# A hybrid SSD backbone on one core: SSD layer ends with the norm factor in PSUM and sums on TensorE, low parts on VectorE alone, step widths a unit later, projections first

## The chip, the cores and the metric

The kernel runs on one core of one Trainium2 chip. The metric is the device time of one execution in microseconds (us); a comparison uses the median of several runs. Five engines work side by side, each through its own queue in order: TensorE (PE, with its weight load PEld), VectorE (DVE), ScalarE (ACT), GpSimd (POOL) and SyncE (SP), which here issues the DMAs of the weights. An engine waits at a semaphore until what it needs is there, and whatever stands behind the waiting instruction on that engine waits too.

## What is computed

The reference is a backbone of four layers with 256 latent and 256 context tokens of width 1024. Each layer modulates a normalised input, runs a mixer (layer 0 and 3: SSD; 1: gMLP; 2: retention), adds it back with a gate, and does the same with a SwiGLU FFN. The context is carried through the first three layers and read, but not written, by the last. Of layer 0's and 3's mixer this matters here:

```python
def rmsnorm(x, g):
    y = xf * lax.rsqrt(jnp.mean(xf * xf, axis=-1, keepdims=True) + EPS)
    return (y * g).astype(x.dtype)
...
z, xbc, dt = jnp.split(h @ w_in, [SSD_INNER, SSD_INNER + SSD_CONV_DIM], axis=-1)
xbc = jax.nn.silu(dwconv(xbc, conv_w, conv_b))
dt_f = jax.nn.softplus(dt[..., :SSD_HEADS] + dt_bias_f)      # the step widths
...
y = y + d_skip * xs                                            # after the scans
y = y.reshape(...) * jax.nn.silu(z)                            # the gate
return rmsnorm(y, norm_g) @ w_out
```

What follows the mixer in every layer is `x = x + g1 * o`, then `modulate(rmsnorm(x, norm2_g), sh2, sc2)` into the FFN.

## The kernel before

**Tiles and products.** Activations lie with the feature on the partition and the token along the row: `X` holds 8 blocks (m = 0 to 7) of 128 features by 512 tokens, the context in columns 0 to 255, the latents from T = 256 on. Every product in float32 is made as three matmuls of a reduced form: a high part `AH` and a low part `AL` of the input, `whi` and `wlo` of the weight; `mm3` issues hi x hi (L307), lo x hi (L308) and hi x lo (L309). A *unit* is one weight block of 128 x 1024 (some of 768): SyncE brings it as `st` (512 KB), ScalarE casts it to `whi` (L227), and a subtraction gives `wlo` (L228). This subtraction runs on VectorE, or on GpSimd for every fourth unit (`POOL_SHARE`, `share[0]`; `boundary` sets other shares by its argument `pool_share`): 372 and 130 units of 502 where the tile is `wlo`. Four units are held in parts at a time. A unit needs 24 matmuls: 8 blocks times three.

**Jobs and quanta.** A job is one unit's matmuls and the evacuation of its PSUM tile. In `boundary`, which joins two stages, the last product of a mixer is cut into quanta of 12 matmuls over 256 tokens, one for each block m of the context (k = 0 to 7) and then of the latents (k = 8 to 15), so that norm, sums and evacuation can be written between them. All PSUM tiles come from one ring of eight banks.

**A norm.** `Norm.add` squares a block of X on ScalarE (L520, L532), and adds it to `nacc` (L526) on GpSimd, the late ones on VectorE. `rms_steps` then makes the factor in three steps: `s0` sums over the partitions on TensorE (L484), takes the mean on VectorE (L488) and the power -1/2 on GpSimd (L489); `s1` puts it on a diagonal `dg` (L494, VectorE); `s2` broadcasts it with a matmul of ones (L498). `Norm.steps` applies it, block by block: a product on VectorE (`t1k`, L557), ScalarE's `AH` (L567), VectorE's `AL` (L551); for the context's m = 0, 2, 4 GpSimd makes AL (L565).

**An SSD layer** (`ssd`, a function inside the kernel's scope) opens with the units of `dt`, B, C and x. `a1` transposes the step widths' input `DX` on TensorE (L865; `dx` is its name); `a2` starts with two VectorE steps (L875, L876) and then runs the softplus as a chain of 21 GpSimd steps (L877 to L889), whose last but one writes `SF` in the trace's names; `dtb` turns it into decays with TensorE's L897, L899, L903. `conv_evac` makes the 5-tap convolutions (ScalarE L821, VectorE L824, four passes) and SiLU (L833). Then four groups follow. In group g, the windows of `WINDOWS` set the order of projections x (for group g+1), z units, and `o` units (the out product of the group before, whose input `yg` comes from the gate: L1061 on TensorE, L1065 and L1072 on VectorE, L1077 on ScalarE, L1089 and L1090), and `scan_slots` puts the scan's steps between them.

**An SSD layer's end.** The sum of squares of the gated y is known only with group 3. So `out_last` computes the out product without the factor, `o_whole` adds it to the earlier groups' part (L1155), `rms_steps` makes the factor `rb`, `rsink` copies it to a tile `th` (L1206, ScalarE), and `o_norm` applies it: `X * g * rb` (L1165, VectorE), then adds the saved x (`back`, L1166, VectorE), then `fin_norms[a].add`. `last.after` says behind which quantum k each of these stands.

**The V scaling of gMLP** (L1264) multiplies the normalised V on VectorE; TensorE's spatial product L1283 waits for it.

Of the kernel before, what the change touches and what calls it, by code (L numbers as in the profile page):

```python
# [16 lines left out]
P = 128  # L17
# [13 lines left out]
POOL_SHARE = 4  # L31

PAD_W, PAD_H = 24, (48, 32)
# [37 lines left out]
class Job:  # L71
# [14 lines left out]
    True: ("zxxzxzxzxx", "oxoxozoxzxzxzx", "oxoxozoxzxzxzx", "zzzozooo"),  # L86
    False: ("zxxzxzxzxx", "oxoxozoxzxzxzx", "oxoxozoxzxzxzx", "zzzozooo"),
# [26 lines left out]
def backbone(ctx, tc, A, out):  # L114
# [44 lines left out]
    MHALF = cp.tile([P, 4 + PAD_W], F32, name="MHALF")[:, :4]  # L159
# [26 lines left out]
    share = [POOL_SHARE]  # L186
# [15 lines left out]
    def emit_split(upto):  # L202

        while at["split"] < min(upto, at["stop"]):
# [23 lines left out]
            (pool if i % share[0] == 0 else dve).tensor_tensor(lo[:, :n], t[:, :n], f32(hi[:, :n]), op=SUB)  # L228
# [197 lines left out]
    def mod_rows(pt):  # L426
        r = tmp(T, "nsq", 3)
        act.copy(r, pt[:, :256])
        return r
# [43 lines left out]
    def rms_steps(acc, n0, n1, dim, sink):  # L473
# [5 lines left out]
        def s0():  # L479
            pt = psm()  # L480
            accs = acc() if callable(acc) else [acc]
            for c in range(nch):
                for k, x in enumerate(accs):
                    pe.matmul(pt[:, c:c + 1], x[:, c * P:(c + 1) * P], one_col,  # L484
                              start=(k == 0), stop=(k == len(accs) - 1))
# [16 lines left out]
    class Norm:  # L502
# [7 lines left out]

        def sums(self):
            return [self.acc] + self.hold

        def add(self, m, eng=pool):

            n = self.n1 - self.n0
            x = X[:, m, self.n0:self.n1]
            if self.acc is None:
# [12 lines left out]
            t = tmp(T, "nsq", 3)[:, :n]  # L531
# [3 lines left out]
        def steps(self, place=None):  # L535
# [6 lines left out]
            pooled = place is None and n0 == 0  # L542
# [76 lines left out]
    def boundary(last, norms, nxt, ranges, hooks=None, lend=(), pool_share=1):  # L619
# [3 lines left out]
        if last is not None:  # L623
            Q = open_job(last)
            if len(ranges) == 1:
                share[0] = pool_share

            def after(k):
                for s_ in last.after.get(k, ()):
                    s_()  # L630
            for k, q in enumerate(Q[:KT]):
                q()
                after(k)
            share[0] = pool_share
            if len(ranges) == 2:
                c = norms[0].steps()
                plan = {1: c[0:2], 2: c[2:5], 3: c[5:7], 4: c[7:9], 5: c[9:10], 6: c[10:]}
                norms[T].later = []
                for k, q in enumerate(Q[KT:]):
                    hold[0] = k >= 4  # L640
                    q()
                    for s_ in plan.get(k, ()):
                        s_()
                    after(KT + k)
                hold[0] = False
                share[0] = len(stream) + 1
# [1219 lines left out]
```

## Time and profile before

| | us |
|---|---|
| median of 3 runs | 2917.42 (2916.7 to 2919.46) |
| the profiled execution's own time | 2919.43 |
| its span in the profile | 2917.7 |
| TensorE busy | 2829.5 (97%) |
| VectorE busy | 1926.9 (66%) |
| ScalarE busy | 1095.0 (38%) |
| GpSimd busy | 526.6 (18%) |

By the lines that run, layer 0's SSD lies at 0 to 556 us of the span, its FFN to 899, gMLP to 1200, its FFN to 1561, retention to 1995, its FFN to 2361, layer 3's SSD to 2713 and its FFN to 2909. The share of the span that an engine is busy says which engine is near its limit on the whole. Where the end moves is read from what TensorE waits for, which is listed by line and by the instruction that released it, and from the granted clock, the share of full speed that TensorE got in a stretch. A group's row in the page gives the count, the busy time and the mean of one.

### The profile page before, as it was taken

What the parts mean: (1) busy time and instruction counts of PE and PEld (TensorE: products, weight loads), DVE (VectorE), ACT (ScalarE), POOL (GpSimd) and SP (SyncE); (2) the same over time, 40 slices, a digit from 0 to 9 for tenths busy, and PEclk for the clock granted to TensorE, in tenths of its full rate; (3) what the DMA queues carried; (4) which work ended last, traced back from release to release, by engine and by line L of the source; (5) the groups of instructions that cost most, each with busy time, mean ns of one, the idle gap of its engine ahead of it and who ended that gap; (6) DMA issues with size and microseconds to landing.
All of it is one profiled execution on the core that took longest, in us unless ns stands there. A gap on an engine that the chain in (4) does not pass through costs nothing. (4 is left out here: it accounts for less than half of the span.)

```text
span 2917.7 us, 40723 instructions
## 1 busy us (share of the span) xinstructions
PE 2829.5 (97%) x16132; PEld 2392.1 (82%) x16132; DVE 1926.9 (66%) x3049; ACT 1095.0 (38%) x1934; POOL 526.6 (18%) x405
## 2 busy tenths in 40 slices
PE   6999999899999999999999999999999999999898
PEld 4777877788889878988889777778888897888898
DVE  4877767688885155587777344345877778888544
ACT  4555444422224422422224322234322245554443
POOL 1311112211112010211113111112111133122222
PEclk9999999999999999999999999999999999999899
DMA  6322223255553222354543222213544522223454
GB/s 216 122 87 102 87 98 127 85 193 199 186 188 116 94 73 89 107 186 174 181 174 115 80 72 87 80 65 109 195 175 173 179 95 87 87 97 120 138 179 139
DMA packets 111678, 376.37 MB, mean 129 GB/s; under 512 B 12160, under 2 KB 16640, under 8 KB 111488
## 3 DMA queue, kind: packets, MB, share of 16 engines
q1 hardware_dynamic: 109296, 367.23, 36.2%
q0 software_dynamic: 1616, 5.77, 0.6%
q8 instruction: 127, 2.08, 0.3%
q10 hardware_dynamic: 576, 0.77, 0.1%
q14 instruction: 63, 0.52, 0.1%
HBM read 369.53 MB, written 4.19 MB: 128 GB/s over the span
## 5 line engine op out<-in xcount | busy, mean ns | idle before, releaser
L307 PE MATMUL mm<-AH,whi 128*128 128x512 f32 (+1 forms) x2456 | 888.9, 362 | 2.0 <-ACT AH L567 1.1
L308 PE MATMUL mm<-AL,whi 128*128 128x512 f32 (+1 forms) x2456 | 881.6, 359 | 0.4 <-DVE AL L1090 0.4
L309 PE MATMUL mm<-AH,wlo 128*128 128x512 f32 (+1 forms) x2456 | 879.7, 358 | 0.0
L227 ACT CAST whi<-st 128x1024 fp32r<-128x1024 f32 (+1 forms) x502 | 503.5, 1007 | 356.1 <-PE mm L308 225.1
L228 DVE TENSOR_TENSOR wlo<-st,whi 128x1024 fp32r<-128x1024 f32 (+1 forms) x372 | 453.7, 1224 | 257.4 <-ACT whi L227 257.2
L228 POOL TENSOR_TENSOR wlo<-st,whi 128x1024 fp32r<-128x1024 f32 (+1 forms) x130 | 322.9, 2484 | 1505.1 <-ACT whi L227 1497.3
L307 PEld LDWEIGHTS mm<-AH,whi 128*128 128x128 f32 x2456 | 465.0, 189 | 80.0 <-issue 4.4
L308 PEld LDWEIGHTS mm<-AL,whi 128*128 128x128 f32 x2456 | 464.6, 189 | 70.6 <-issue 1.2
L309 PEld LDWEIGHTS mm<-AH,wlo 128*128 128x128 f32 x2456 | 464.5, 189 | 68.9
L413 DVE SCALAR_TENSOR_TENSOR mj<-mst,cb 128x1024 bf16<-128x1024 f32 x304 | 439.6, 1446 | 39.5 <-DMA mst<-in_mod_w_dram 33.5
L585 DVE SCALAR_TENSOR_TENSOR X<-mm,MOD,X 128x256 f32<-128x256 f32 x332 | 147.9, 478 | 132.7 <-PE mm L309 132.7
L307 PE MATMUL mm<-hh,whi 128*128 128x512 f32 (+1 forms) x576 | 210.7, 366 | 0.0
L309 PE MATMUL mm<-hh,wlo 128*128 128x512 f32 (+1 forms) x576 | 209.8, 364 | 0.0
L308 PE MATMUL mm<-hl,whi 128*128 128x512 f32 (+1 forms) x576 | 208.1, 361 | 0.0
L307 PE MATMUL mm<-yg,whi 128*128 128x256 f32 (+1 forms) x592 | 198.7, 336 | 6.1 <-ACT yg L1089 4.7
L308 PE MATMUL mm<-yg,whi 128*128 128x256 f32 (+1 forms) x592 | 192.0, 324 | 1.5 <-DVE yg L1090 1.2
L309 PE MATMUL mm<-yg,wlo 128*128 128x256 f32 (+1 forms) x592 | 191.7, 324 | 0.0
L1562 ACT CAST hh<-s 128x512 fp32r<-128x512 f32 (+1 forms) x72 | 40.8, 567 | 297.1 <-DVE s L1552 297.1
L1552 DVE TENSOR_TENSOR s<-s,mm 128x512 f32<-128x512 f32 (+1 forms) x88 | 54.6, 620 | 130.6 <-PE mm L309 130.6
L307 PEld LDWEIGHTS mm<-yg,whi 128*128 128x128 f32 x592 | 112.5, 190 | 18.1 <-ACT yg L1089 5.3
L1534 ACT ACTIVATE s<-mm 128x512 f32<-128x512 f32 (+1 forms) x88 | 47.9, 544 | 202.4 <-PE mm L309 201.9
L309 PEld LDWEIGHTS mm<-hh,wlo 128*128 128x128 f32 x576 | 107.9, 187 | 19.0
(362 smaller groups left out, 4053.3 us busy)
## 6 DMA issues: line engine op xcount, KB each, us to landing
st<-in_ffn_w_dram SPq DMA_DIRECT2D x176, 512.0 KB, 3.3
mst<-in_mod_w_dram SPq DMA_DIRECT2D x152, 512.0 KB, 4.2
st<-in_ssd_in_dram SPq DMA_DIRECT2D x82, 512.0 KB, 3.3
st<-in_ffn_w2a_dram SPq DMA_DIRECT2D x96, 384.0 KB, 3.0
st<-in_ssd_out_dram SPq DMA_DIRECT2D x32, 512.0 KB, 3.3
st<-in_ret_in_dram SPq DMA_DIRECT2D x32, 512.0 KB, 3.2
st<-in_mod_n_dram SPq DMA_DIRECT2D x24, 512.0 KB, 3.9
st<-in_ffn_w2b_dram SPq DMA_DIRECT2D x16, 512.0 KB, 3.5
```

Of the source, the lines that this page charges most:

```text
L227: act.copy(hi[:, :n], t[:, :n])
L228: (pool if i % share[0] == 0 else dve).tensor_tensor(lo[:, :n], t[:, :n], f32(hi[:, :n]), op=SUB)
L307: pe.matmul(pt, lh, rh, start=(start and i == 0), stop=False)
L308: pe.matmul(pt, lh, rl, start=False, stop=False)
L309: pe.matmul(pt, ll, rh, start=False, stop=(stop and i == n - 1))
L413: dve.scalar_tensor_tensor(j, t, 1.0, mp[1][:, v], op0=MUL, op1=MUL, accum_out=MOD[:, i, v, ct:ct + 1])
L585: dve.scalar_tensor_tensor(X[:, m, a:b], pt[:, a - n0:b - n0], g, X[:, m, a:b], op0=MUL, op1=ADD)
L1534: act.activation(t[:, :b - a], pt, AF.Silu)
L1552: dve.tensor_tensor(s, s, pt, op=MUL)
L1562: act.copy(hh[:, a:b], s)
```

## The change

The diff does five things.

1. **Low parts.** All subtractions of L228 go to VectorE; `POOL_SHARE`, `share` and `pool_share` are gone.
2. **The SSD end.** The factor stays in its PSUM tile (`rb[0] = pt`, no copy to `th`). The add of `back` moves to GpSimd. The three steps of the factor stand behind quanta 1, 2, 3 (layer 0; before 1, 3, 4) and 0, 1, 2 (layer 3; before 0, 2, 3), the applications accordingly earlier. For the first norm behind an SSD layer (context in layer 0, latents in layer 3), `direct` is set: each square is summed on TensorE, by two matmuls with `PICK` (a column of ones among zeros) into one PSUM tile, by `pump`, which leaves two squares waiting. In layer 0 the context's norm steps stand one quantum later, and low parts of further units are held back from quantum 5 on in layer 3. In layer 3 the latents' norm lets GpSimd make AL for m = 0, 2, 4 (`shared`).
3. **Step widths.** `a1` and `a2` stand one step later, and `dtb` moves from the end of the x projections to the first slot of group 0, so behind the first z unit.
4. **Windows.** Those of groups 1 and 2 begin with `x` ("xooxo...") and not with `o` ("oxoxo...").
5. **Tiles.** `nsq` has four buffers for three, DX shares the tag `xs`, and paddings change (`PAD_H`), as do labels of PSUM tiles in the FFN, which share one ring all the same.

The core of the diff:

```diff
-            (pool if i % share[0] == 0 else dve).tensor_tensor(lo[:, :n], t[:, :n], f32(hi[:, :n]), op=SUB)
+            dve.tensor_tensor(lo[:, :n], t[:, :n], f32(hi[:, :n]), op=SUB)
...
-    True: ("zxxzxzxzxx", "oxoxozoxzxzxzx", "oxoxozoxzxzxzx", "zzzozooo"),
+    True: ("zxxzxzxzxx", "xooxozoxzxzxzx", "xooxozoxzxzxzx", "zzzozooo"),
...
+        def pump(self, keep=2):
+            while self.direct and len(self.pend) > keep:
+                t = self.pend.pop(0)
+                if self.pt is None:
+                    self.pt = ps("s")
+                for c in range(2):
+                    pe.matmul(self.pt[:, :2], t[:, c * P:(c + 1) * P], PICK[:, 1 - c:3 - c],
+                              start=(self.done == 0 and c == 0), stop=(self.done == KT - 1 and c == 1))
+                self.done += 1
...
+            if self.direct:
+                t = tmp(T, "nsq", 4)[:, :n]
+                act.activation(t, x, AF.Square)
+                self.pend.append(t)
+                return
...
+                if last.after:
+                    plan = {2: c[0:2], 3: c[2:5], 4: c[5:7], 5: c[7:9], 6: c[9:10], 7: c[10:]}
...
-                        dve.tensor_tensor(x, x, back[m][:, a:b], op=ADD)
+                        pool.tensor_tensor(x, x, back[m][:, a:b], op=ADD)
...
-                      sk_units[:3], sk_ev, prep, {(3, 0): [a1], (3, 1): [a2]})
+                      sk_units[:3], sk_ev, prep, {(3, 1): [a1], (3, 2): [a2]})
...
-            run(rest, [[]] * (len(rest) - 1) + [[dtb]])
+            run(rest)
...
-                    slots = scan_slots(g)
+                    slots = ([[dtb]] if g == 0 else []) + scan_slots(g)
...
-                        rb[0] = tmp(512, "th", 2)[:, lo:]
-                        act.copy(rb[0], pt)
+                        rb[0] = pt
...
-                last.after = {0: rms[0:1], 2: rms[1:2], 3: rms[2:3], "end": [o_norm(8)]}
-                last.after.update({k: [o_norm(2)] for k in (4, 5, 6, 7)})
+                last.after = {0: rms[0:1], 1: rms[1:2], 2: rms[2:3], 6: [o_norm(1)], "end": [o_norm(8)]}
+                last.after.update({k: [o_norm(2)] for k in (3, 4, 5)})
+            fin_norms[lo].direct = True
```

Three places show how instructions move. The first is VectorE in the opening of layer 0: `bt` and `ct` are the convolutions of B and C, `vps` the two steps that release GpSimd's chain of step widths, `wlo` low parts. Before:

```order
L228 TENSOR_TENSOR wlo_522<-st_507,whi_521 128x1024
L867 SCALAR_TENSOR_TENSOR C_126_535<-E_534 128x256
L824 SCALAR_TENSOR_TENSOR bt_557<-y_355,cw_95,bt_557 128x2x254
L824 SCALAR_TENSOR_TENSOR bt_557<-y_355,cw_95,bt_557 128x2x255 x2
L824 SCALAR_TENSOR_TENSOR bt_557<-y_355,cw_95,bt_557 128x2x254
L875 TENSOR_SCALAR vps_536<-C_126_535 128x256
L876 RECIPROCAL vps_536<-vps_536 128x256
L228 TENSOR_TENSOR wlo_591<-st_511,whi_590 128x1024
L824 SCALAR_TENSOR_TENSOR ct_604<-mm_362,cw_95,ct_604 128x2x254
```

And now (the changed kernel numbers its lines otherwise: L854 is L824, L897 is L867, L905 and L906 are L875 and L876, L227 is L228):

```order
L227 TENSOR_TENSOR wlo_537<-st_511,whi_536 128x1024
L854 SCALAR_TENSOR_TENSOR bt_548<-y_357,cw_97,bt_548 128x2x254
L854 SCALAR_TENSOR_TENSOR bt_548<-y_357,cw_97,bt_548 128x2x255 x2
L854 SCALAR_TENSOR_TENSOR bt_548<-y_357,cw_97,bt_548 128x2x254
L897 SCALAR_TENSOR_TENSOR C_130_555<-E_554 128x256
L227 TENSOR_TENSOR wlo_566<-st_513,whi_565 128x1024
L854 SCALAR_TENSOR_TENSOR ct_579<-mm_364,cw_97,ct_579 128x2x254
L854 SCALAR_TENSOR_TENSOR ct_579<-mm_364,cw_97,ct_579 128x2x255 x2
L854 SCALAR_TENSOR_TENSOR ct_579<-mm_364,cw_97,ct_579 128x2x254
L905 TENSOR_SCALAR vps_556<-C_130_555 128x256
L906 RECIPROCAL vps_556<-vps_556 128x256
L227 TENSOR_TENSOR wlo_621<-st_527,whi_620 128x1024
```

The two steps on `vps` stood ahead of the convolutions of C and now stand behind them and behind one more low part.

The second is TensorE where layer 0's projections end and group 0 begins: `SF` is the step widths' result. Before:

```order
L307 MATMUL mm_735<-AH,whi_618 128x512
L308 MATMUL mm_735<-AL,whi_618 128x512
L309 MATMUL mm_735<-AH,wlo_619 128x512
L897 MATMUL y_767<-SF_109,CST 128x128 x4
L899 MATMUL g_772<-SF_109,CST 128x256
L903 MATMUL g_774<-CST,SF_109 32x128 x8
L307 MATMUL mm_809<-AH,whi_658 128x512
L308 MATMUL mm_809<-AL,whi_658 128x512
```

And now:

```order
L306 MATMUL mm_777<-AH,whi_660 128x512
L307 MATMUL mm_777<-AL,whi_660 128x512
L308 MATMUL mm_777<-AH,wlo_661 128x512
L927 MATMUL y_806<-SF_111,CST 128x128 x4
L929 MATMUL g_811<-SF_111,CST 128x256
L933 MATMUL g_813<-CST,SF_111 32x128 x8
L969 MATMUL y_839<-CST,bt_548 128x128 x2
L974 MATMUL g_844<-ct_579,bt_548 128x128 x4
```

The unit that followed the three products on SF (the first z unit, 24 matmuls) stands ahead of them now, and the scan's first products follow them.

The third is VectorE in the last quanta of layer 3's out product. Before:

```order
L1155 TENSOR_TENSOR X<-mm_22797,X 128x256
L1165 SCALAR_TENSOR_TENSOR X<-X,MOD,th_22737 128x256
L1166 TENSOR_TENSOR X<-X,AL 128x256
L1165 SCALAR_TENSOR_TENSOR X<-X,MOD,th_22737 128x256
L1166 TENSOR_TENSOR X<-X,AL 128x256
L1155 TENSOR_TENSOR X<-mm_22821,X 128x256
L1165 SCALAR_TENSOR_TENSOR X<-X,MOD,th_22737 128x256
L1166 TENSOR_TENSOR X<-X,AL 128x256
L526 TENSOR_TENSOR nacc_22761<-nacc_22761,nsq_22819 128x256
L1165 SCALAR_TENSOR_TENSOR X<-X,MOD,th_22737 128x256
L1166 TENSOR_TENSOR X<-X,AL 128x256
L526 TENSOR_TENSOR nacc_22761<-nacc_22761,nsq_22838 128x256
```

And now (L1185 is L1155, L1195 is L1165, L490 is L488):

```order
L1185 TENSOR_TENSOR X<-mm_22754,X 128x256
L1195 SCALAR_TENSOR_TENSOR X<-X,MOD,s_22724 128x256 x2
L1185 TENSOR_TENSOR X<-mm_22776,X 128x256
L1195 SCALAR_TENSOR_TENSOR X<-X,MOD,s_22724 128x256 x2
L1185 TENSOR_TENSOR X<-mm_22803,X 128x256
L1195 SCALAR_TENSOR_TENSOR X<-X,MOD,s_22724 128x256
L1185 TENSOR_TENSOR X<-mm_22825,X 128x256
L1195 SCALAR_TENSOR_TENSOR X<-X,MOD,s_22724 128x256
L490 TENSOR_SCALAR ms_22851<-s_22790 128x2
L496 TENSOR_SCALAR dg_22855<-CST,rs_22852 128x128 x2
```

The adds of `AL` and the sums into `nacc` are gone from VectorE, the factor is read from a PSUM tile `s`, and the next norm's mean stands right behind the last product.

## Rows read from the trace of the kernel before

**Rows 1.** The page: busy us, share and instructions; groups: count | busy, mean ns.
```profile
PE 2829.5 (97%) x16132; PEld 2392.1 (82%) x16132; DVE 1926.9 (66%) x3049; ACT 1095.0 (38%) x1934; POOL 526.6 (18%) x405
...
L228 DVE TENSOR_TENSOR wlo<-st,whi 128x1024 fp32r<-128x1024 f32 (+1 forms) x372 | 453.7, 1224 | 257.4 <-ACT whi L227 257.2
L228 POOL TENSOR_TENSOR wlo<-st,whi 128x1024 fp32r<-128x1024 f32 (+1 forms) x130 | 322.9, 2484 | 1505.1 <-ACT whi L227 1497.3
...
L585 DVE SCALAR_TENSOR_TENSOR X<-mm,MOD,X 128x256 f32<-128x256 f32 x332 | 147.9, 478 | 132.7 <-PE mm L309 132.7
```

**Rows 2.** TensorE's waits, whole span: line, releaser: us in total, times, longest.
```profile
PE y L897 <- POOL SF L888: 8.1, 2, 5.9
...
PE mm L307 <- ACT yg L1089: 4.7, 2, 3.0
...
PE s L865 <- ACT dx L844: 2.9, 2, 2.1
...
PE y L1283 <- DVE V L1264: 2.6, 4, 0.8
```

**Rows 3.** The same view, 480 to 560 us (end of layer 0).
```profile
PE mm L484 <- DVE nacc L526: 5.8, 1, 5.8
PE mm L484 <- POOL nacc L526: 4.8, 1, 4.8
```

**Rows 4.** The same view, 2680 to 2725 us (end of layer 3).
```profile
PE mm L484 <- DVE nacc L526: 7.8, 1, 7.8
PE s L498 <- DVE dg L494: 4.0, 2, 2.4
```

**Rows 5.** Stretches: length; busy PE, PEld, DVE, ACT, POOL; granted clock; DMA.
```profile
518.40:525.20 6.80, 6.80 (x31) 6.62 (x32) 3.33 (x10) 1.34 (x4) 0.71 (x1) 0.50 0.00 0
538.80:545.70 6.90, 5.67 (x26) 5.67 (x27) 5.12 (x9) 3.25 (x4) 0.71 (x1) 0.51 0.34 106
1030.40:1037.20 6.80, 6.33 (x16) 4.98 (x17) 4.94 (x9) 1.57 (x2) 0.00 (x0) 0.50 0.00 0
2412.80:2419.60 6.80, 4.04 (x22) 3.25 (x24) 5.80 (x11) 3.00 (x4) 5.72 (x5) 0.50 0.00 0
2487.80:2491.30 3.50, 3.12 (x15) 3.10 (x15) 2.18 (x3) 2.31 (x6) 0.07 (x1) 0.51 0.19 44
2692.60:2696.10 3.50, 3.50 (x16) 3.34 (x16) 1.27 (x2) 1.32 (x2) 0.00 (x0) 0.51 1.03 390
2702.90:2720.00 17.10, 9.24 (x35) 7.99 (x36) 12.28 (x27) 6.08 (x12) 3.95 (x4) 0.50 0.09 32
```

**Rows 6.** The same view, three long stretches (FFN 0, layer 3, FFN 3).
```profile
556.00:880.00 324.00, 324.00 (x1450) 267.06 (x1450) 259.40 (x363) 87.55 (x111) 44.50 (x16) 1.00 0.52 184
2360.00:2680.00 320.00, 306.70 (x2392) 277.57 (x2391) 270.79 (x479) 167.48 (x364) 82.74 (x89) 0.98 0.26 90
2730.00:2900.00 170.00, 170.00 (x1437) 170.00 (x1437) 85.18 (x117) 75.71 (x109) 39.98 (x20) 1.00 0.54 178
```

**Rows 7.** Timeline of GpSimd, 58 to 96 us: start, length, what [idle before].
```profile
70.52 1.60 POOL L877 TENSOR_TENSOR vpo<-C,vps 128x256 f32<-128x256 f32 x1 [4.13 <-DVE vps L876]
...
89.26 0.72 POOL L888 TENSOR_TENSOR SF<-xtok,ea 128x256 f32<-128x256 f32 x1
```

**Rows 8.** Timeline of VectorE, the same stretch.
```profile
71.44 3.08 DVE L824 SCALAR_TENSOR_TENSOR ct<-mm,cw,ct 128x508 f32<-128x508 f32 x4
```

**Rows 9.** Timeline of VectorE, 2683 to 2716 us.
```profile
2701.49 0.43 DVE L1166 TENSOR_TENSOR X<-X,AL 128x256 f32<-128x256 f32 x1
...
2702.34 2.44 DVE L1166 TENSOR_TENSOR X<-X,AL 128x256 f32<-128x256 f32 x1
```

**Rows 10.** Timeline of GpSimd, the same stretch.
```profile
2702.05 2.46 POOL L228 TENSOR_TENSOR wlo<-st,whi 128x1024 fp32r<-128x1024 f32 x1 [0.88 <-ACT whi L227]
```

**Rows 11.** Timeline of VectorE, 1018 to 1034 us (gMLP).
```profile
1024.60 7.01 DVE L1264 TENSOR_SCALAR V<-V,rsv 128x2048 f32<-128x2048 f32 x4 [1.12 <-POOL rsv L1260]
```

**Rows 12.** Timeline of GpSimd, 514 to 549 us (end of layer 0).
```profile
517.42 0.79 POOL L526 TENSOR_TENSOR nacc<-nacc,nsq 128x256 f32<-128x256 f32 x1 [0.94 <-ACT nsq L532]
```

More of the change, by code (lines that the diff above doesn't have):

```diff
@@ L479, in s0 @@
         def s0():
-            pt = psm()
             accs = acc() if callable(acc) else [acc]
[L482 to L485, printed above, removed]
+            if isinstance(accs, tuple):
+                pt, = accs
+            else:
+                pt = psm()
+                for c in range(nch):
+                    for k, x in enumerate(accs):
+                        pe.matmul(pt[:, c:c + 1], x[:, c * P:(c + 1) * P], one_col,
+                                  start=(k == 0), stop=(k == len(accs) - 1))
             ms = sp.tile([P, 4], F32, tag="ms", name=nm("ms"), bufs=3)
@@ L509, in __init__ @@
             self.later = None
+            self.direct = False
+            self.pend, self.pt, self.done = [], None, 0
+            self.shared = n0 == 0
         def sums(self):
+            if self.direct:
+                self.pump(0)
+                assert self.done == KT
+                return (self.pt,)
             return [self.acc] + self.hold
+        def pump(self, keep=2):
[7 more added lines that the diff above has]
+                self.done += 1
         def add(self, m, eng=pool):
@@ L541, in steps @@
             step = KT if place is None else 2
-            pooled = place is None and n0 == 0
+            pooled = place is None and self.shared
             def sink(pt):
@@ L630, in after, with pump @@
                     s_()
+            def pump():
+                for a, _ in ranges:
+                    norms[a].pump()
             for k, q in enumerate(Q[:KT]):
+                hold[0] = len(ranges) == 1 and k >= 5 and bool(last.after)
                 q()
+                pump()
                 after(k)
-            share[0] = pool_share
             if len(ranges) == 2:
@@ L650, in boundary @@
                     f()
+            if len(ranges) == 1 and last.after:
+                norms[T].shared = True
             lt = norms[T].steps()
@@ L1218, in ssd @@
             if need_ctx:
[L1219 to L1225 removed]
+                last.after = {1: rms[0:1], 2: rms[1:2], 3: rms[2:3], "end": [o_norm(8)]}
+                last.after.update({k: [o_norm(2)] for k in (4, 5, 6, 7)})
+                last.after.update({k: [o_norm(1)] for k in range(8, 16)})
+            else:
+                last.after = {0: rms[0:1], 1: rms[1:2], 2: rms[2:3], 6: [o_norm(1)], "end": [o_norm(8)]}
+                last.after.update({k: [o_norm(2)] for k in (3, 4, 5)})
+            fin_norms[lo].direct = True
             return last, yr
```

43 lines of the change are left out of this document (18 added, 25 removed).

## The prediction

> **What bounds the kernel now.** I read the page first: TensorE is busy 2829.5 of 2917.7 us [rows 1], so in the long stretches nothing but its own matmuls sets the time, and a change that leaves their number alone can win only from the 88 us in which it is idle and from stretches in which it runs at the lower clock. So I went next to TensorE's waits, over the whole span and then by stretch [rows 2 to 4], and then to the granted clock of the stretches that follow these waits [rows 5]. The reader is to see two things. The waits sit in a few places: the opening of each SSD layer (the step widths `SF`, 2.2 us in layer 0 and 5.9 in layer 3, and `dx`, 2.1 and 0.8), the start of its group 1 (`yg`, 1.7 and 3.0), its end (the sums of squares, 4.8 and 5.8 in layer 0, 7.8 in layer 3, where the broadcast of a factor takes 4.0 more), and gMLP's scaling of V (2.6). And behind most of these a stretch follows at a granted clock of 0.50, which is the lower of the two levels, 1.2 against 2.4 GHz. TensorE's work there takes twice its time: half of its busy time in such a stretch is lost. A unit of 24 matmuls of 512 columns takes 24 x 324.0/1450 = 5.4 us, one of 256 columns 24 x 170.0/1437 = 2.8, a quantum of 12 of these 1.4 [rows 6].
>
> **The change part by part.** The sum is made against the profiled execution's own time, 2919.4, which is 2.0 above the median of 2917.4.
>
> *Low parts all on VectorE.* 130 units of 502 go from GpSimd (2.48 us each) to VectorE (1.22) [rows 1]: about 130 x 1.2 = 156 us more for an engine that is busy two thirds of the time. What speaks for no cost is what the two engines do to each other: an add that took 0.43 us at 2701.49 took 2.44 at 2702.34, and a GpSimd low part of 2.46 had begun at 2702.05 [rows 9, 10]; the four V scalings took 7.01 where one low part of GpSimd lay beside them [rows 11]. VectorE gets part of the added time back there. The densest stretch, the FFN with the modulation steps, has VectorE busy 259.4 of 324 us while TensorE never waits; layer 3's scans have 270.8 of 320 [rows 6]. 16 GpSimd instructions lie in the first, all of them low parts: 16 x 1.2 = 19 more still fits in 324. On TensorE's path: 0, between -6 (a lost hand-over of 0.4 us in fifteen places, no row shows it) and +2. Its one direct gain is gMLP: the V scaling no longer shares with a low part, so most of the 2.6 of wait goes, and with it the clock stretch of 6.8 us with 6.33 busy, half of which is 3.2 [rows 2, 5]. Gain 5 (1.9 if the clock still falls, 5.8 if all goes).
>
> The Trainium skill (SBUF — State Buffer, "Who interferes with whom") says that a VectorE instruction with two SBUF inputs contends with a GpSimd instruction that reads SBUF, the later one being blocked for the other's whole length, and that one with a single SBUF input does not. The rows agree (0.43 became 2.44 beside a low part; L585, which reads PSUM and SBUF, has a mean of 478 ns over 332). The rule also speaks against this change, since it puts 24 adds that read SBUF on GpSimd beside VectorE's low parts; that is the first rival.
>
> *Hooks and step widths, layer 0.* The dx wait (2.1) goes, since another projection step stands ahead of the transposes. But VectorE's two steps that release GpSimd's chain of widths now stand behind the four C convolutions (3.08) and one low part (1.22) [rows 8], as the first place of the order shows: the chain, 70.52 to 89.98 [rows 7], starts 4.3 later, and SF comes at about 94.2. TensorE asked for it at 87.8; it is there 2.1 earlier now, but has a z unit of 5.4 ahead: 91.1, so it waits 3.1 where it waited 2.2. What was over at 90.0 + 5.4 = 95.4 is over at 94.2. The rest of the opening is bound by VectorE, so I take 0.5 (-4 to +4).
>
> *The same, layer 3.* z is 256 columns wide, so 2.8 of the 5.9 [rows 2] are covered, and the dx wait of 0.8 goes. The chain is issued a quantum (1.4) later. The clock stretch of 6.8 with 4.04 busy loses 2.0 now [rows 5]; part of it may go. Gain 4: 2.8 + 0.8 + 1.4 of the clock, less 1.0 for the chain. Ends: 2 and 6.
>
> *Groups 2 and 3 open with a projection.* In the code these are the windows of groups 1 and 2: the x unit stands ahead of the output unit that needs `yg`. Its 5.4 us cover the gate chain whole: waits of 1.7 and 3.0, and in layer 3 the clock (3.12/2 = 1.6) [rows 2, 5]. Gain 1.7 (1 to 2.5) and 4.6 (3 to 5).
>
> *End of layer 0.* Lost now: 4.8 + 5.8 of waits [rows 3], half of 6.80 and of 5.67 busy, 3.4 + 2.8 [rows 5]: 16.8. The context's sums go to TensorE: 32 small matmul records instead of 8; priced like matmuls of 256 columns (0.118), an upper end, 2.8 more. The latents' squares are still summed on GpSimd, which now has 16 adds and 4 sums at 0.79 [rows 12] and three AL parts besides, 18 us, in about 22 us of quanta: I leave a wait of 3.5 before the latents' factor, 0.8 in small ones, and a clock stretch of half the present losses, 3. 16.8 - 10.1 = 6.7; I take 6.5 (3, if the clock falls twice as now, to 12).
>
> *End of layer 3.* Lost now: 7.8 + 4.0 of waits [rows 4], half of 3.50 and of 9.24 busy, 1.8 + 4.6 [rows 5]: 18.2. VectorE loses 8 adds of 0.42 and two sums, GpSimd takes them at 0.79, so two in a quantum (1.6) just miss TensorE's 1.4. What remains, by estimate: the 4.0 of the two broadcasts, whose three steps on three engines stay; 1.1 of a last chain of multiply (0.48), add (0.79), square and pick; 3.7 because the first AL parts come one by one, some from GpSimd at 0.79 now (between 0 and 8 x 0.79 = 6.3); 2.8 for the small matmuls: 11.6. Of the 6.6 left I take 6 (3, if the clock falls again for three fifths of the time it does now, to 10).
>
> Sum: 5 + 0.5 + 4 + 1.7 + 4.6 + 6.5 + 6 = 28.3, and 2919.4 - 28.3 = 2891.1 for the profiled kind of run, 2.0 less for the median: **2889**.
>
> **The rivals.**
> *The SSD ends give nothing.* The adds on GpSimd and the low parts on VectorE block each other, one collision costing up to 2.0 us (0.43 to 2.44); with four or five of them per end the last square is as late as now, and the clock falls as now. For it: 24 adds, and more low parts on VectorE than before. Against: at the ends the low parts are held back while the adds run. It takes 12.5 from the sum: 2889 + 12.5 = 2902.
> *All waits and half-clock stretches at these places go.* The gaps left are short, and some gaps of about 2 us now are followed by no slower stretch (the 2.2 before SF in layer 0). Then the ends give 12 + 10, gMLP 5.8, layer 3's opening 6, group starts 7.5, layer 0's 2: 43, so 2874.
> *Slower: VectorE becomes the engine that is last.* Its queue is in order, and a low part of 1.22 us that stood on GpSimd now stands ahead of an evacuation for which TensorE waits. 156 us of VectorE time are added. If more than 28/156, under a fifth, falls on TensorE's path, the gain is gone; with 0.3 of it, 47 us, the time is 2917 + 19 = 2936. The place would be the FFN with the modulation steps and the scans of layer 3 [rows 6]. Against it: in the first, TensorE does not wait at all with VectorE at 80%, and the low part is taken from an engine whose low part held VectorE up.
> *It moves waits only.* The step widths arrive later than the unit put ahead covers, VectorE's late low parts eat the gMLP gain, and the ends return little: 2913 to 2922.
>
> **How the numbers follow.** Forecast (a gain of 20 to 36) 0.62, first rival 0.17, all waits gone 0.10, waits moved only 0.07, slower by VectorE 0.04. A measurement of this kernel tells about 0.2%, 5.8 us, from no change. Faster by more than that: 0.62 + 0.17 + 0.10 = 0.89, and 0.01 of the moved waits: 0.90; within 0.2%: 0.06; slower: 0.04. The range takes in the forecast's own 2881 to 2897, the first rival's 2902 and the edge of the case in which all goes, 2874: 2873 to 2904, which leaves out somewhat under 2 in 10.
>
> **What would show it.** In the profile after: TensorE's waits for `yg` and for V's scale gone, granted clock 1.00 around 1030 and at group 1 of layer 3; a wait for SF of 3 to 5 in layer 0 and of about 3 in layer 3; no wait of 7.8 at the end of layer 3 but several of 1 to 2; VectorE's busy time up by 60 to 130 us, less than the 156 that it takes over; the mean of its low part near 1.22. I am wrong if TensorE shows many new waits of some tenths for VectorE in the FFNs, if GpSimd's adds show up as releasers at the SSD ends with waits as long as now, or if the clock falls in places where it does not now.

## The result and the profile after

The changed kernel takes 2887.34 us (median of 4 runs, 2883.62 to 2890.18) where the kernel before took 2917.64 beside it: a ratio of 0.9895, 95% interval 0.9878 to 0.9912. The forecast was 2889, in a range of 2873 to 2904. The profiled execution took 2887.09 with a span of 2885.3, so its span is 32.4 us shorter than before.

The page of the changed kernel, its busy times and the groups that answer to those of [rows 1] (L227 is L228 of before, L412 the sums of the modulation steps, L413 of before), and behind it L413 from the page before:

```profile
PE 2822.3 (98%) x16180; PEld 2392.1 (83%) x16180; DVE 1926.2 (67%) x3150; ACT 1092.8 (38%) x1935; POOL 220.7 (8%) x294
...
L227 DVE TENSOR_TENSOR wlo<-st,whi 128x1024 fp32r<-128x1024 f32 (+1 forms) x502 | 588.7, 1177 | 317.2 <-ACT whi L226 316.9
...
L412 DVE SCALAR_TENSOR_TENSOR mj<-mst,cb 128x1024 bf16<-128x1024 f32 x304 | 371.2, 1221 | 21.8 <-DMA mst<-in_mod_w_dram 16.3
```

```profile
L413 DVE SCALAR_TENSOR_TENSOR mj<-mst,cb 128x1024 bf16<-128x1024 f32 x304 | 439.6, 1446 | 39.5 <-DMA mst<-in_mod_w_dram 33.5
```

VectorE now makes all 502 low parts, 135 us more of them (588.7 against 453.7), and is busy for 1926.2 us where it was 1926.9. GpSimd is busy 306 us less. Half of the added work was paid back by one group: L412's 304 instructions took 439.6 us before (a mean of 1446 ns) and take 371.2 now. Not all of the rest is paid back by faster instructions: the change also takes 24 adds and some sums off VectorE, and with the low parts moved alone (`b_low` below) its busy time rises by 15.8.

TensorE's waits, whole span, to be held against [rows 2]:

```profile
PE y L927 <- POOL SF L918: 7.3, 2, 4.4
...
PE mm L486 <- DVE nacc L552: 6.5, 3, 5.3
...
PE s L531 <- ACT nsq L541: 1.9, 1, 1.9
PE mm L306 <- ACT AH L590: 1.6, 1, 1.6
PE y L1312 <- DVE V L1293: 1.3, 2, 0.7
```

The waits for the gate's `yg` (4.7) and for `dx` in layer 3 are gone, that for `dx` in layer 0 has fallen from 2.1 to 0.8 (its tile is `xs` now), V's has halved, and of the 18.4 us for the sums of squares at the SSD ends (5.8 + 4.8 + 7.8, [rows 3, 4]) 5.3 are left, and 1.9 for a square that TensorE now sums itself. Stretches of the trace after, as in [rows 5] (length; busy us of PE, PEld, DVE, ACT, POOL; granted clock; DMA share, GB/s):

```profile
526.70:533.50 6.80, 6.50 (x30) 6.51 (x31) 4.29 (x7) 4.00 (x5) 1.77 (x3) 0.50 0.43 132
1011.00:1031.00 20.00, 18.69 (x93) 15.48 (x92) 14.88 (x24) 4.93 (x7) 0.18 (x1) 1.00 0.23 80
2393.80:2400.60 6.80, 4.64 (x26) 3.50 (x26) 6.48 (x9) 3.87 (x6) 2.79 (x4) 0.50 0.24 83
2455.00:2475.00 20.00, 20.00 (x147) 17.63 (x146) 18.03 (x27) 11.21 (x23) 0.80 (x2) 1.00 0.24 79
2670.30:2687.30 17.00, 13.67 (x57) 12.56 (x58) 7.59 (x19) 7.22 (x16) 5.14 (x8) 0.50 0.00 0
```

gMLP (second row) and the start of layer 3's group 1 (fourth) run at the full clock; the end of layer 0 has one slow stretch where it had two, and layer 3's end has one of the same 17 us.

How far each place had come, from the start of the same instruction in both traces:

| start of | before | after | earlier by | gained since the row above | forecast |
|---|---|---|---|---|---|
| first L1155, layer 0's out product | 498.9 | 491.7 | 7.2 | 7.2 | 0.5 + 1.7 = 2.2 |
| last L585 of layer 0's FFN (65th in the trace) | 908.6 | 895.5 | 13.1 | 5.9 | 6.5 |
| first L585 of gMLP (66th) | 1058.0 | 1040.5 | 17.5 | 4.4 | 5 |
| L865 of layer 3 (dx) | 2388.1 | 2368.7 | 19.4 | 1.9 | 0 |
| first L1155 of layer 3 | 2688.4 | 2658.6 | 29.8 | 10.4 | 4 + 4.6 = 8.6 |
| last L585 | 2904.9 | 2872.6 | 32.4 | 2.6 | 6 |

### The profile page after: what moved, and what is told of

Same layout as the page of the kernel before. It is cut to its first block, busy times and chain, and to the rows that moved or that the text cites. A ratio compares the mean times of both kernels' runs of the same rounds, so it can differ in the third digit from the quotient of the medians.

```text
span 2885.3 us, 40761 instructions
## 1 busy us (share of the span) xinstructions
PE 2822.3 (98%) x16180; PEld 2392.1 (83%) x16180; DVE 1926.2 (67%) x3150; ACT 1092.8 (38%) x1935; POOL 220.7 (8%) x294
## 4 chain that ended last, share of the span: by engine, by line
PE 83%; DVE 6%; issue 6%; ACT 3%; POOL 2%; DMA 0%; POOLq 0%; DVEq 0%; ACTq 0%; SPq 0%
PE mm L306 24%; PE mm L308 24%; PE mm L307 24%; PE y L1091 2%; DVE wlo L227 1%; PE s L1019 1%; PE g L1448 1%; PE g L1063 1%; PE g L1065 1%; DVE AL L577 1%; ACT whi L226 0%; PE y L1312 0%; PE y L1466 0%; PE y L1465 0%; PE s L500 0%
## 5 line engine op out<-in xcount | busy, mean ns | idle before, releaser
L227 DVE TENSOR_TENSOR wlo<-st,whi 128x1024 fp32r<-128x1024 f32 (+1 forms) x502 | 588.7, 1177 | 317.2 <-ACT whi L226 316.9
L412 DVE SCALAR_TENSOR_TENSOR mj<-mst,cb 128x1024 bf16<-128x1024 f32 x304 | 371.2, 1221 | 21.8 <-DMA mst<-in_mod_w_dram 16.3
L307 PEld LDWEIGHTS mm<-hl,whi 128*128 128x128 f32 x576 | 108.7, 189 | 16.9
```

The costliest lines, as they stand in the source:

```text
L227: dve.tensor_tensor(lo[:, :n], t[:, :n], f32(hi[:, :n]), op=SUB)
L307: pe.matmul(pt, lh, rl, start=False, stop=False)
L412: dve.scalar_tensor_tensor(j, t, 1.0, mp[1][:, v], op0=MUL, op1=MUL, accum_out=MOD[:, i, v, ct:ct + 1])
```

## Experiments: one part undone at a time

My theory was the sum of the prediction; its rivals said that the SSD ends give nothing, or that VectorE becomes the engine that is last. All kernels were timed beside the kernel before, on one chip per set; a difference to the changed kernel is the difference of the two ratios times 2917.6. The two intervals together leave such a difference open by some 6 us either way; where it is smaller, the time settles nothing, and the reading rests on the waits and starts of the traces, one profiled run of each kernel.

**Low parts on GpSimd again** (`u_share`).

```diff
-            dve.tensor_tensor(lo[:, :n], t[:, :n], f32(hi[:, :n]), op=SUB)
+            (pool if i % share[0] == 0 else dve).tensor_tensor(lo[:, :n], t[:, :n], f32(hi[:, :n]), op=SUB)
```

> The changed kernel with one part undone: low parts go to GpSimd again for every fourth unit, with the shares at the boundaries as before. Theory (GpSimd's low parts hold VectorE up, most of all in gMLP's scaling of V, and nothing is lost where VectorE takes them): the 4.4 us that gMLP gained and the 2.7 that came bit by bit between the gMLP and layer 3 go, and the SSD ends get a low part of 2.4 us on GpSimd ahead of its adds: 2887 + 7 to 12 = 2894 to 2899, V's scaling at over 5 us for four again. Rival (the low parts on VectorE cost something that the other parts of the change hide): 2887 or less, down to 2880. GpSimd busy time goes from 221 to about 530 us in either.

Measured: 2906.51 us, a ratio of 0.9954 (0.9940 to 0.9968), so 17 us above the changed kernel and well above the 7 to 12 expected. gMLP's scaling of V is slow again, with the one low part beside it (the timeline of VectorE, this kernel and then the changed one: start, length, what [idle before]):

```profile
1015.63 7.01 DVE L1304 TENSOR_SCALAR V<-V,rsv 128x2048 f32<-128x2048 f32 x4 [1.12 <-POOL rsv L1300]
```

```profile
1011.21 4.87 DVE L1293 TENSOR_SCALAR V<-V,rsv 128x2048 f32<-128x2048 f32 x4 [1.12 <-POOL rsv L1289]
```

But about half (9.2 of the 18.8 us between the two traces, by the starts of the same instructions) is lost in layer 3 at a wait that neither theory had. The waits of TensorE in this kernel, and GpSimd's timeline at that place, layer 3's opening:

```profile
PE mm L310 <- POOL wlo L229: 9.3, 1, 9.3
...
PE y L938 <- POOL SF L929: 2.4, 1, 2.4
```

```profile
2402.72 0.79 POOL L929 TENSOR_TENSOR SF<-xtok,ea 128x256 f32<-128x256 f32 x1
2403.60 0.84 POOL L930 TENSOR_SCALAR xtok<-xtok 128x256 f32<-128x256 f32 x1
2404.41 2.34 POOL L229 TENSOR_TENSOR wlo<-st,whi 128x1024 fp32r<-128x1024 f32 x1
```

The low part at 2404.41 is that of the z unit which the change puts ahead of the decays to cover GpSimd's chain. With its low part on GpSimd it stands behind that very chain, and TensorE waits 9.3 us for it instead of 4.4 for SF. So the two parts are not independent: in layer 3 the decays' move pays only because no low part is on GpSimd.

**Windows opening with the out unit again** (`u_win`).

```diff
-    True: ("zxxzxzxzxx", "xooxozoxzxzxzx", "xooxozoxzxzxzx", "zzzozooo"),
+    True: ("zxxzxzxzxx", "oxoxozoxzxzxzx", "oxoxozoxzxzxzx", "zzzozooo"),
```

(and the same for `False`).

> The changed kernel with the windows of groups 1 and 2 opening with an out unit again. Theory (the x unit covers the gate chain): TensorE waits for yg again, about 2.5 in layer 0 and 3.4 in layer 3 with a stretch at half clock behind it; of the 3.0 and 7.5 us that the traces show as gained at these two places, all goes: 2897 (2894 to 2900). Rival (a good part of these gains came from VectorE being freer, not from the order): +3, 2890, and waits for yg under 1.5 us.

Measured: 2898.73, ratio 0.9935 (0.9923 to 0.9948), 11.7 above the changed kernel. TensorE's wait in layer 3's group 1 (2440 to 2480 us) and the stretch behind it:

```profile
PE mm L306 <- ACT yg L1119: 4.0, 1, 4.0
```

```profile
2468.50:2475.30 6.80, 5.85 (x25) 5.56 (x26) 3.38 (x6) 4.26 (x9) 0.73 (x1) 0.50 0.22 80
```

In layer 0 the wait is 1.7 again. The theory holds; the price of the two places is larger than the waits of [rows 2], since the half clock comes on top (5.85/2 = 2.9). These make 1.7 + 4.0 + 2.9 = 8.6 of the 11.7; the rest lies within what the intervals leave open.

**Step widths as before** (`u_hooks`).

```diff
-                      sk_units[:3], sk_ev, prep, {(3, 1): [a1], (3, 2): [a2]})
+                      sk_units[:3], sk_ev, prep, {(3, 0): [a1], (3, 1): [a2]})
...
-            run(rest)
+            run(rest, [[]] * (len(rest) - 1) + [[dtb]])
```

(layer 3's hooks and the slots of group 0 go back likewise).

> The changed kernel with the step widths as before: the transposes and the chain a step earlier, the decays at the end of the x projections. Theory: layer 0 waits 2.1 for dx and about 2 for SF, layer 3 about 0.8 and 5 to 6 for SF; the 2.0 us that layer 0 and the 2.2 that layer 3 gained there go: 2891 (2889 to 2894). Rival (the opening is bound by VectorE, so the order of the step widths is worth nothing): 2887.

Measured: 2891.84, ratio 0.9906 (0.9892 to 0.9919), 3.2 above the changed kernel, in the theory's range, though the intervals overlap and the rival's 2887 is not excluded by the time. The waits are back as the theory had them, 2.6 for SF and 2.1 for dx more than in the changed kernel:

```profile
PE y L927 <- POOL SF L918: 9.9, 2, 6.8
...
PE s L895 <- ACT xs L874: 2.9, 2, 2.2
```

**SSD ends as before** (`u_end`): the copy of the factor, the adds on VectorE, `direct` and `shared` off, the old schedule, the old places of the context's norm and no low parts held back.

> The changed kernel with the SSD ends as before: factor copied to SBUF, adds on VectorE, squares summed on GpSimd and VectorE, the old schedule. Low parts stay on VectorE. Theory (the end's own rewriting brought the 5.1 us of layer 0 and the 3.2 of layer 3): 2887 + 8 = 2895 (2892 to 2899), waits of 4 to 6 at each of layer 0's sums and of 6 to 8 at layer 3's. Rival (the ends gained because GpSimd has no low parts there any more): +2, 2889, and layer 3's wait for its sums at 4 or less.

Measured: 2892.95, ratio 0.9912 (0.9898 to 0.9925), 5.0 above the changed kernel, at the lower edge of the theory and with overlapping intervals. TensorE's waits at the end of layer 0 (480 to 560 us), then at the end of layer 3 (2640 to 2700):

```profile
PE mm L486 <- DVE nacc L552: 5.7, 1, 5.7
PE mm L486 <- POOL nacc L552: 4.8, 1, 4.8
```

```profile
PE mm L486 <- DVE nacc L552: 9.1, 1, 9.1
PE s L500 <- DVE dg L496: 2.3, 2, 1.5
```

The waits are back in full, so the rival, by which GpSimd's low parts caused them, falls. Yet by the starts of the same instructions the rewriting is worth 5.0 us in layer 0 and 1.5 in layer 3, where a wait of 9.1 comes back: layer 3's end is where a large change moves the time little. I come back to it below.

The four undone parts cost 17.2, 11.7, 3.2 and 5.0, together 37.1, while the whole change gave 30.6. The excess is not clear of the noise by the times; the traces point to the pair found above, and two parts alone on the kernel before test it.

## Experiments: parts alone, and the pair

**Low parts alone** (`b_low`, the kernel before with the one line changed).

> The kernel before with one part of the change alone: all low parts on VectorE. Undoing this part in the changed kernel cost 17 to 19 us, 9.3 of it in one wait of TensorE in layer 3's opening, for a low part that stood on GpSimd behind the chain of step widths. Theory (that wait arises only because the z unit now goes ahead of the decays; the part alone is worth the rest): 2917.6 - 8 = 2910 (2907 to 2912), gMLP's wait for V halved and its half-clock stretch gone. Rival (GpSimd's low parts cost 17 by themselves): 2900 to 2902.

Measured: 2907.25, ratio 0.9962 (0.9948 to 0.9975), so 11.1 below the kernel before, between the two, nearer to the theory. The rows of its page and of its waits that answer to what the two engines do to each other:

```profile
PE 2821.9 (97%) x16132; PEld 2388.8 (82%) x16132; DVE 1942.7 (67%) x3179; ACT 1098.7 (38%) x1934; POOL 206.0 (7%) x275
...
L413 DVE SCALAR_TENSOR_TENSOR mj<-mst,cb 128x1024 bf16<-128x1024 f32 x304 | 371.5, 1222 | 21.8 <-DMA mst<-in_mod_w_dram 16.5
```

```profile
PE y L1283 <- DVE V L1264: 1.4, 2, 0.7
```

VectorE's busy time is 1942.7 us where it was 1926.9: of the 136 us of added low parts 120 are paid back by other instructions, L413 with 68 of them. By the starts of the same instructions 1.9 of the gain are made by layer 0's dx (TensorE's first wait for AH falls from 4.0 to 2.8 there), 4.6 in gMLP, 2.5 from there to layer 3's dx, and 2.3 at layer 3's end, where the 2.44 us add of [rows 9] was.

**Step widths alone** (`b_hooks`, the kernel before with hooks and decays moved as in the change).

> The kernel before with the step widths' part alone: transposes and chain a step later, decays behind the first z unit; a quarter of the low parts stays on GpSimd. Theory (the z unit's low part stands on GpSimd's queue behind the chain of 21 steps, so the unit put ahead to cover the chain waits for the chain's end itself): TensorE waits 8 to 10 us for a low part of GpSimd in layer 3 in place of the 5.9 for SF, the gain in the changed kernel (3 to 5) does not come: 2915 to 2920. Rival (the unit covers as it does in the changed kernel): 2913 or less, wait for SF of 3 to 4.5 in layer 3.

Measured: 2919.29, ratio 1.0006 (0.9997 to 1.0014): nothing, where undoing it in the changed kernel costs some 3. The wait and its cause are those of `u_share`:

```profile
PE mm L309 <- POOL wlo L228: 9.3, 1, 9.3
```

So the 17 of the low parts in the changed kernel are, in the medians, 11 of their own and about 6 for making room for the step widths' move. The intervals alone would leave these 6 open; the starts show the pair where the wait is. From layer 3's dx to its first L1155 the low parts alone gain 0.4 us and undoing them in the changed kernel loses 9.2; the step widths' move loses 5.4 while GpSimd still makes low parts and gains 2.5 once it makes none.

## Experiments: what is left at the places that gained less

**Adds on VectorE again** (`e_dve`): one word in `o_norm`, `pool` to `dve` for the add of `back`.

> The changed kernel with the 24 adds of the SSD ends on VectorE again (8 in layer 3, 16 in layer 0), all else as changed. Theory (at these ends VectorE is the engine behind which squares and sums wait, and each add there costs it 0.42): the wait for the latents' sum in layer 0 grows from 5.3 to 6 to 8, layer 3's picks come later: 2888 to 2891. Rival (an add takes 0.74 on GpSimd against 0.42, and the hand-over to it and back is longer than what VectorE saves): 2883 to 2886.

Measured: 2885.71, ratio 0.9889 (0.9872 to 0.9905), the same as the changed kernel's within the intervals, and the wait for layer 0's sum is shorter, not longer (480 to 560 us):

```profile
PE mm L486 <- DVE nacc L552: 4.7, 1, 4.7
```

The theory is wrong here: no part of the gain shows for the move of the 24 adds (by the starts, layer 0's end is 0.5 longer without it and layer 3's 2.0 shorter). An add takes 0.74 on GpSimd and 0.42 on VectorE, and VectorE, busy for 1936.4 us in this kernel, had the time.

**Layer 0's end** (`v_l0`). In the changed kernel's timeline of VectorE the latents' last multiply (L1195) stands behind the last steps of the context's norm, whose AL waits for ScalarE, and the sums behind it:

```profile
524.87 0.48 DVE L577 SCALAR_TENSOR_TENSOR AL<-t1k,MOD,AH 128x256 fp32r<-128x256 f32 x1 [0.60 <-ACT AH L593]
525.27 0.47 DVE L1195 SCALAR_TENSOR_TENSOR X<-X,MOD,s 128x256 f32<-128x256 f32 x1
525.66 1.28 DVE L552 TENSOR_TENSOR nacc<-nacc,nsq 128x256 f32<-128x256 f32 x2
```

```diff
+                    if k == 7:
+                        after(KT + k)
                     for s_ in plan.get(k, ()):
                         s_()
-                    after(KT + k)
+                    if k < 7:
+                        after(KT + k)
...
-            plan = {1: lt[0:1], 2: lt[1:2], 4: lt[2:5], 5: lt[5:7], 6: lt[7:9], 7: lt[9:]}
+            plan = {2: lt[0:2], 4: lt[2:5], 5: lt[5:7], 6: lt[7:9], 7: lt[9:]}
```

> The changed kernel with two moves at the boundaries with two token ranges: behind the last quantum of the out product VectorE's multiply for the latents' last block stands ahead of the last step of the context's norm and not behind it, and the latents' sum stands one quantum of the next job later. Theory (the 5.3 us for which TensorE waits at the end of layer 0 is VectorE's order, and a quantum of 2.8 can stand before it): the wait falls to 0 to 1.5, and the half-clock stretch of 6.8 behind it is gone: 2887.3 - 5 to 8 = 2879 to 2882. Rival (the latents' norm is late by as much for the quanta that need it, at all three boundaries with two ranges): 2886 to 2890.

Measured: 2884.27, ratio 0.9882 (0.9868 to 0.9895), 3.8 below the changed kernel, though the intervals overlap; by the starts of the same instructions layer 0's end gives 1.1 of it. TensorE's waits at 480 to 560 us, and the stretch that still follows:

```profile
PE mm L306 <- ACT AH L593: 1.8, 2, 0.9
...
PE mm L486 <- DVE nacc L552: 0.3, 1, 0.3
```

```profile
528.90:535.70 6.80, 6.78 (x32) 6.78 (x32) 5.15 (x7) 2.53 (x3) 2.01 (x3) 0.50 0.61 201
```

The wait of 5.3 is gone, but two of 0.9 for AH, one of 0.4 for AL and the 0.3 left for the sum stand in its place between 524.5 and 528.9, and the clock falls all the same for 6.8 us. That half of the expectation failed: short waits, 2.5 us in all, were enough here for what the long one did.

**Layer 3's end** (`v_hold`). Here the changed kernel shows a low part for which VectorE waits 2.54 us, and the evacuation that TensorE's next step needs stands behind it:

```profile
2662.91 0.86 DVE L1195 SCALAR_TENSOR_TENSOR X<-X,MOD,s 128x256 f32<-128x256 f32 x2
2666.31 1.22 DVE L227 TENSOR_TENSOR wlo<-st,whi 128x1024 fp32r<-128x1024 f32 x1 [2.54 <-ACT whi L226]
2667.45 0.42 DVE L1185 TENSOR_TENSOR X<-mm,X 128x256 f32<-128x256 f32 x1
```

```diff
-                hold[0] = len(ranges) == 1 and k >= 5 and bool(last.after)
+                hold[0] = len(ranges) == 1 and k >= 3 and bool(last.after)
```

> The changed kernel with one number changed: in layer 3's last product the splits are held back from quantum 3 on and not from 5. Theory (one low part there waits for its cast, which stands on ScalarE behind two squares, and VectorE's evacuation and two multiplies stand behind it, so the sums reach TensorE 1.9 us late and the half-clock stretch of 17 us begins there): the wait of 1.9 goes, the stretch begins some 8 us later or is shorter: 2887.3 - 2 to 5 = 2882 to 2885. Rival (the stretch comes anyhow, from the hand-overs of the norm behind it, and a unit that is split later is late for the FFN): 2886 to 2890.

Measured: 2888.7, ratio 0.9897 (0.9883 to 0.9910): nothing. The rows say why (TensorE's waits; the broadcast of the next norm's factor, here and then in the changed kernel; the slow stretch):

```profile
PE mm L306 <- ACT whi L226: 2.4, 1, 2.4
...
PE s L531 <- ACT nsq L541: 1.1, 1, 1.1
```

```profile
2677.22 0.70 PE L500 MATMUL s<-dg,CST 128*128 128x256 f32 x2 [1.55 <-DVE dg L496]
```

```profile
2678.89 1.22 PE L500 MATMUL s<-dg,CST 128*128 128x256 f32 x2 [1.55 <-DVE dg L496]
```

```profile
2678.00:2691.60 13.60, 9.02 (x37) 8.14 (x38) 9.18 (x16) 8.99 (x15) 2.19 (x3) 0.50 0.25 80
```

Counted from the first evacuation of the out product (2661.4 here, 2658.6 there) the factor comes after 15.8 instead of 20.3 us, so 4.5 are won; the last L585 comes after 213.9 against 214.0. They are given back by the wait for the held unit (2.4) and by the slow stretch, which now lies over the FFN's first quanta. Kernels with this end as in the changed one and a slow stretch of the same 13.7 us take 212.5 (`v_h0` below), so against them the hold costs 1.4. The slow stretch follows the next norm's hand-overs too (1.55 and 1.55), so no single wait of this end carries it. What would take it away I have not found.

**The two openings** (`v_x0`, `v_h0`).

```diff
-    False: ("zxxzxzxzxx", "xooxozoxzxzxzx", "xooxozoxzxzxzx", "zzzozooo"),
+    False: ("xzxzxzxzxx", "xooxozoxzxzxzx", "xooxozoxzxzxzx", "zzzozooo"),
```

> The changed kernel with one window changed: layer 3's group 0 opens with an x unit (512 columns, 5.4 us) and not with a z unit (256 columns, 2.8), so the decays stand behind the longer one. Theory (the 4.4 us for which TensorE still waits for SF there is the chain's length less what stands ahead): the wait falls to 1.5 to 2, the half-clock stretch of 6.8 is gone or shorter: 2887.3 - 3 to 5 = 2882 to 2885. Rival (the group's scan, whose first steps then come 2.6 later under the same units, gives it back as a wait for E or for the gate): 2886 to 2889.

Measured: 2888.98, ratio 0.9899 (0.9884 to 0.9913), nothing. The 2380 to 2480 us of its waits, whole, where the changed kernel has 4.4 for SF:

```profile
PE mm L306 <- DVE bt L854: 3.7, 1, 3.7
PE y L927 <- POOL SF L918: 1.7, 1, 1.7
```

The wait for SF fell by the 2.7 that the longer unit covers, and the z unit behind it now waits 3.7 for a PSUM tile that VectorE's convolution of that unit still reads: the rival, with another releaser than it named.

```diff
-                      sk_units[:3], sk_ev, prep, {(3, 1): [a1], (3, 2): [a2]})
+                      sk_units[:3], sk_ev, prep, {(3, 0): [a1], (3, 1): [a2]})
```

> The changed kernel with layer 0's two hooks a step earlier, as before the change; layer 3's and the decays' place stay. Theory (VectorE's two steps that start the chain stand ahead of the convolutions of C again, so SF is there 3 to 4 us earlier and the wait of 2.8 for it goes, while the wait of 2.1 for dx comes back): 2887.3 + 0 to -2 = 2885 to 2888. Rival (the later hooks were worth the dx wait and its clock, and VectorE is what bounds the opening): 2889 to 2892.

Measured: 2884.72, ratio 0.9888 (0.9874 to 0.9903), 2.0 below the changed kernel, inside the theory and inside the noise:

```profile
PE y L927 <- POOL SF L918: 4.5, 1, 4.5
...
PE s L895 <- ACT xs L874: 2.1, 1, 2.1
```

Layer 0's wait for SF (2.8) is gone and the one for dx is back, as forecast, and layer 0's first L1155 starts 3.2 us earlier (488.5). By this trace the decays' late place was the good half of that part in layer 0, the later hooks the bad one.

**All four together** (`v_best2`).

> The changed kernel with four things together: layer 3's group 0 opening with x, layer 0's hooks a step earlier, and the two moves at the boundaries with two ranges (the latents' last multiply ahead of the context's last norm step, their sum a quantum later), which gave 3 to 4 us by themselves. Theory (these places are apart in time and the gains add): 2884 - 3 to 5 - 0 to 2 = 2877 to 2881. Rival (what is gained ahead of a stretch that VectorE or the weights bound is given back there): 2882 to 2886.

Measured: 2882.21 (2881.72 to 2886.68), ratio 0.9879 (0.9865 to 0.9894). It is the fastest kernel of this study and clear of the kernel before; that it beats the changed kernel (0.9878 to 0.9912) is likely but not settled. It lies 1 above the theory's range, less than the noise; the x unit's part gave nothing by itself.

## Why the prediction was right, and where its terms were off

The direction, the places and the total were right: 28.3 forecast, 30.6 measured in the median and 32.4 in the profiled runs. The terms were not equally good, and that the total came so near is in part luck: the opening and the first group starts of layer 0 gave 5.0 more than forecast, layer 3's opening and group start 1.8 more and the stretch between gMLP and layer 3 1.9 where nothing was expected, while layer 3's end gave 3.4 less.

*Low parts.* The mechanism was right and its size too small. The term was 5, all of it for gMLP, where 4.4 came. Alone the part is worth 11. The rest was set at 0 between -6 and +2: in fact it gained, 1.9 by layer 0's dx, 2.5 between gMLP and layer 3, 2.3 at layer 3's end. I had priced the added work (156) and only said that some would come back; VectorE's busy time, forecast to rise by 60 to 130, rose by 15.8 in `b_low` and, with the adds and sums off VectorE too, fell by 0.7 in the changed kernel. The rival in which VectorE becomes the bound is refuted by these rows and by the time. The rule of the Trainium skill on which I leaned (SBUF — State Buffer, "Who interferes with whom") agrees with these runs: L412, whose two large inputs lie in SBUF, went from 1446 to 1221 ns once GpSimd's low parts were gone, while L585 (PSUM and SBUF) stayed at 478. One row falls outside the rule as the prediction gives it: V's scaling has one large SBUF input, and still its four instructions took 7.01 us beside a low part and 4.87 without. The Trainium skill exempts, in that section, a single SBUF input only outside the two-port modes, which the prediction left out. That V's scaling runs in such a mode is likely (1.28 us for 2048 columns, where a low part takes 1.22 for 1024) but not shown.

*Step widths.* In layer 0 I had SF at 94.2 and a wait of 3.1; TensorE got it at 91.2 after a wait of 2.8, so the opening gave 90.0 + 5.4 - 91.2 = 4.2 and not 0.5; 1.9 of that comes with the part above (in `b_low` TensorE gets SF at 88.1 where it got it at 90.0). In layer 3 the wait left is 4.4 against 3.1 forecast, and the slow stretch behind it stayed, so 1.5 + 0.8 of waits came for the 4. What I missed altogether is that the two parts hang together through GpSimd's queue: I asked what is queued behind each moved step on VectorE, and did not ask whose low part stands behind the chain on GpSimd. With the low parts there the move is worth nothing (`b_hooks`): 2.5 us gained by layer 0's first L1155 and 5.4 lost in layer 3.

*Windows.* 6.3 forecast, 11.7 by undoing. The waits were covered as forecast. The term was too small because it took layer 3's from the kernel before: without the cover it is 4.0 in `u_win` against 3.0, and the slow stretch behind it 6.8 against 3.5. This makes the term 8.6; the rest of the 11.7 is not accounted for, and not clear of the noise.

*End of layer 0.* 6.5 forecast, 5.9 measured (5.0 by undoing). The forecast wait of 3.5 for the latents' sum is 5.3, and one slow stretch of 6.8 is left, as allowed for.

*End of layer 3.* This is the step that failed: 6 forecast, 2.6 in the trace, and 1.5 by undoing the rewriting. The waits went down further than forecast: 7.8 + 4.0 [rows 4] became 1.9 + 2.7, and one for AH grew from 1.1 to 1.6, so 6.7 were won. TensorE's own work took most of it back. From the first evacuation of the out product to the last L585 (as in [rows 5]; before, after, then `v_h0`, in which this end is the same):

```profile
2688.40:2904.90 216.50, 203.61 (x1658) 201.60 (x1656) 116.48 (x176) 93.78 (x140) 54.76 (x31) 0.95 0.50 163
```

```profile
2658.60:2872.60 214.00, 207.46 (x1686) 205.59 (x1684) 127.71 (x185) 94.53 (x143) 12.19 (x17) 0.96 0.49 164
```

```profile
2658.20:2870.70 212.50, 205.97 (x1687) 204.11 (x1685) 127.79 (x185) 94.44 (x143) 12.21 (x17) 0.97 0.50 166
```

TensorE was idle there for 12.9 us and is for 6.5, but it is busy for 3.9 more. The 2.8 for the small matmuls was right as it was meant, at the full clock; most of them stand in the slow stretch (TensorE's timeline of the changed kernel, sums of squares):

```profile
2665.20 0.95 PE L531 MATMUL s<-SMALL,nsq 128*128 128x2 f32 x8
...
2669.57 1.70 PE L531 MATMUL s<-SMALL,nsq 128*128 128x2 f32 x8 [1.90 <-ACT nsq L541]
...
2673.84 3.50 PE L531 MATMUL s<-SMALL,nsq 128*128 128x2 f32 x16
```

They take 6.2 us where eight such took 1.9 (2708.09 to 2709.97 in the trace before). The term that failed is the clock: of the 11.6 that I left, 8.8 were waits, 2.8 the small matmuls and nothing the clock; only the lower end of the range let it fall, for three fifths of its stretch. The waits left are 6.4, less than the 8.8, but the clock falls for the same 17.0 us, with 13.67 of TensorE's work in it, of which half is 6.8; before, 1.8 + 4.6 = 6.4 were lost. So 6.4 of idle time won, less 2.8 for the small matmuls and 0.4 for the clock, is 3.2, near the 2.6 measured. Part of this differs from run to run: in `u_hooks`, `v_l0`, `v_x0`, `v_h0` and `v_best2`, whose end of layer 3 is the same code and has about the same waits, the slow stretch is 13.7 us long and the end gains 4.1; in `u_win` it is 17.1 and 2.6, as in the changed kernel. Why it is longer in some runs stays open. The first rival (ends that give nothing) was half right there, for another reason than its own: `e_dve` shows no effect of the adds on GpSimd either way.

## What to carry to other kernels

Before a unit of work is put ahead to cover a chain, look at which queue prepares that unit: if it is the queue that runs the chain, the cover waits for the chain's end. Work moved onto a busy engine, from one whose instructions slow it down, can cost the busy engine far less than its length (15.8 of 136 us in `b_low`): price what stops colliding as well as what is added, from the means of the groups with and without the overlap. Where a wait is followed by a stretch at the lower clock, do not count the clock as won while short waits are left beside it (`v_l0`), and price what is put into that stretch at the lower clock.

## What the runs showed of the hardware that I had not expected

With 323 us of GpSimd's low parts gone, VectorE took 130 more instructions, 136 us in all, and was busy for only 15.8 us more (`b_low`, 1926.9 to 1942.7). What a wait costs in clock is not in proportion to it: in `v_l0` four waits of 0.3 to 0.9, 2.5 us in all, were followed by the same 6.8 us at a granted clock of 0.50 as one of 5.3 in the changed kernel. And the lower level does not quite double TensorE's time: in the changed kernel's trace twelve matmuls of 256 columns take 2.56 us at 0.50 (2684.34 to 2686.90, by their starts) and 1.41 at 1.00 (2691.34 to 2692.75), 1.8 times as long, so the halves of busy time that the prediction and this text take as lost are about a tenth too high.
